# One weight load split in two, two table loads placed where they are used, and the background steps of the first MLP group dealt out over the later ones

## The chip, the cores and the metric

The kernel runs on 1 core of one Trainium2 chip. The metric is the device time of one execution in microseconds (us). Where several executions were timed, the median is given.

## The reference

Two layers of a mixer block over 512 tokens of width 1024, with a context of 256 tokens ahead of them. The cut below keeps what the change touches: the modulation vectors (six per layer, for the tokens from `c` and for the context from `c_ctx`) and the MLP with its squared ReLU.

```python
for l in range(DEPTH):                       # DEPTH = 2
    need_ctx = l < DEPTH - 1
    mx = jnp.split((jax.nn.silu(c) @ w_ada[l] + b_ada[l])[:, None, :], 6, axis=-1)
    mc = jnp.split((jax.nn.silu(c_ctx) @ w_ada[l] + b_ada[l])[None, None, :], 6, axis=-1)
    hx = modulate(rmsnorm(x, g_pre_mix[l]), mx[0], mx[1])
    hc = modulate(rmsnorm(ctx, g_pre_mix[l]), mc[0], mc[1])
    out_x, out_c = token_mixers(hx, hc, ...)   # mLSTM heads, a Fourier mix, a conv module
    x = x + mx[2] * rmsnorm(out_x, g_post_mix[l])
    hx = modulate(rmsnorm(x, g_pre_mlp[l]), mx[3], mx[4])
    x = x + mx[5] * rmsnorm(sq_relu_mlp(hx, w_mlp1[l], w_mlp2[l]), g_post_mlp[l])
    if need_ctx:
        ...                                    # the same for ctx with mc
def sq_relu_mlp(h, w1, w2):
    return jnp.square(jax.nn.relu(h @ w1)) @ w2
```

## The kernel before

All values are fp32. A product is made from three matmuls on halves: weights and activations are each split into a rounded `hi` (an ACT copy, L220 or L231) and a rest `lo` (a DVE subtraction, L221 or L234). A weight block arrives by DMA in a `raw` tile, is split into `hi` and `lo`, and the raw tile is free again. There are 3 raw tiles, 6 hi, 5 lo, 20 tiles called t3, 8 called t4, and two groups of 4 PSUM banks (`mm` and `aux`).

What sets the order: a scheduler takes the program as written, gives each engine one queue and may move an instruction ahead of others in it. Every engine then runs its queue strictly in order and waits on semaphores. All DMAs that move data are issued by SyncE (SP), in one queue. A DMA into a raw tile waits there until the tile's former content has been read, and what is behind it in the queue waits too.

**The start.** `ada_first` (L281 on) computes the first modulation vectors of layer 0 from four quarters of `w_a0`. Each quarter is loaded into the `rooms` of its row (L290); a room of 128x1024 takes two blocks of the contraction, a room called `half_` takes one, in the first 512 columns of a t3 tile. L313 multiplies the blocks on PE with the silu of the conditions (`csil`). The first part of the layer, meanwhile, runs the value projection of the mLSTM (L511) with weights `w_v`. Behind the loads of the context (`ctx`) stand two DMAs that write `csil` column by column into a small table `cd` in DRAM (L587), and one that loads the table `bd` for the Fourier mix (L588). Nothing reads them soon: `bd` is used at L935, and `cd` is read back by L330.

**The MLP of layer 0** takes 768 tokens, 6 blocks of 128, and 32 blocks of 128 hidden columns in 8 groups of 4. Group 0 is plain: L464 multiplies the hidden blocks, `mlp1_out` squares them (L1063, L1064), L1074 multiplies with the second weights, and ACT evicts the result into 6 accumulators (L1238). Between the evictions DVE builds sums of the activations (`sum_steps`, L1108 to L1130), since groups 1 to 7 use a Strassen-like scheme with two pairs of hidden blocks per group (`mlp1_pair`): seven products of 12 matmuls each (L1143) per pair, combined by DVE (L1162, L1170, L1173, L1179) with copies by ACT (L1158, L1169, L1178, L1184). The evictions of these groups are DVE additions (L1242) into the accumulators.

**The background steps.** Layer 1's modulation vectors are computed on DVE (`ada_dve_steps`), in 52 steps: a start that reads the table `cd` back into two t4 tiles, 48 steps that each load 512 KB of `w_at` into a raw tile (L339) and run multiply-and-reduce instructions over it (L343), and three final steps. The 16 steps of the first third have four L343 instructions each, two of which write their unneeded product into an `aux` bank; the other 32 have two. A call of `background()` takes the next steps from the list, two of them per call (L1316). Group 0 calls it four times behind its products (L1202, L1203); groups 1 to 6 call it four times each, at three places in the products and once ahead of the second product with the second weights.

Of the kernel before, what the change touches and what calls it, by code (L numbers as in the profile page):

```python
# [65 lines left out]
def build(tc, a):  # L66
# [156 lines left out]
    def weight(*key, ahead=AHEAD):  # L223
        assert stream[st["used"]][0] == key, (stream[st["used"]][0], key)
        st["used"] += 1
        prep(st["used"] + ahead)
        return ready.pop(key)
# [55 lines left out]
    def ada_first(res):  # L283
        ac = small.tile([128, 4, 8], F32, tag="ac0", name=nm("ac"))
        res["ac", 0] = ac
        raw_ = lambda: rawp.tile([128, 1024], F32, tag="raw", name=nm("raw"))
        hi_ = lambda: hip.tile([128, 1024], F32, tag="hi", name=nm("raw"))
        lo_ = lambda: lop.tile([128, 1024], F32, tag="lo", name=nm("raw"))
        half_ = lambda: t3()[:, :512]
        rooms = ((raw_, raw_, raw_, t4), (hi_, hi_, hi_, lo_), (lo_, raw_, raw_, raw_), (half_,) * 6 + (raw_,))  # L290
        parts = []
        bt = c2()
        for q in range(4):
            parts.append([])
            kb = 0
            for i, r in enumerate(rooms[q]):
                n = 1 if r is half_ else 2
                raw = r().rearrange("p (k j n) -> p k j n", k=n, j=4)
                dma(raw, a["w_a0"][q, kb // 2] if n == 2 else a["w_a0"][q, kb // 2, :, kb % 2:kb % 2 + 1])
                if q == i == 0:  # L300
                    dma(bt, a["bada"][0, 0])
                for k in range(n):
                    parts[q].append(raw[:, k])
                kb += n
            if q < 3:
                pre["v", 0, 0, q] = t3()[:, :264 * (VKB[q][1] - VKB[q][0])]
                dma(pre["v", 0, 0, q].rearrange("p (k n) -> p k n", n=264), a["w_v"][0, 0, :, VKB[q][0]:VKB[q][1], :])
        yield
        for q in range(4):
            ps = aux()  # L310
            for kb in range(KB):
                for j in range(4):
                    T.matmul(ps[32 * j:32 * j + 32, 0:128], csil[:, kb, :], parts[q][kb][:, j, :],  # L313
                             start=kb == 0, stop=kb == KB - 1, tile_position=(0, 32 * j))
            R = bt[:, 128 * q:128 * q + 128]
            V.tensor_tensor(R, ps[:, 0:128], R, ALU.add)
            yield
            cp = aux()
            T.matmul(cp[:, 0:8], R, sel, start=True, stop=True)
            V.tensor_copy(ac[:, q, :], cp[:, 0:8])  # L320
            yield


    def ada_dve_steps(l, res):
        box = {}

        def start():
            box["c"] = [t4() for _ in range(2)]
            for v in range(2):
                dma(box["c"][v], cd[v].partition_broadcast(128))  # L330

        def step(g, j, cb):
            def run():
                if (j, cb) == (0, 0):
                    box["part"] = small.tile([128, 2, 4, 8], F32, tag="part", name=nm("part"))
                    if g:
                        V.memset(box["part"], 0.0)
                w = rawp.tile([128, 2, 512], F32, tag="raw", name=nm("raw"))
                dma(w, a["w_at"][l - 1, g, j, cb])  # L339
                for v in (1, 0) if g == 0 else (0,):  # L340
                    for i in range(2):
                        o = aux() if v else w[:, i, :]
                        V.scalar_tensor_tensor(o, w[:, i, :], 1.0, box["c"][v][:, 512 * i:512 * i + 512],  # L343
                                               ALU.mult, ALU.mult,
                                               accum_out=box["part"][:, i, cb, 2 * j + v:2 * j + v + 1])
            return run

        def fin(g):
            def run():
                ac = small.tile([128, 4, 8], F32, tag=f"ac{g}", name=nm("ac"))  # L350
                res["ac", g] = ac
                part = box["part"]
                bg_ = small.tile([128, 4, 8], F32, tag="bac", name=nm("bac"))
                dma(bg_, a["bcol"][l - 1, g])
                V.tensor_tensor(ac, part[:, 0], part[:, 1], ALU.add)
                V.tensor_tensor(ac, ac, bg_, ALU.add)
                if g:
                    gp = small.tile([128, 8], F32, tag="gp", name=nm("gp"))
                    dma(gp, a["gpcol"][l - 1, g - 1])
                    jv = ac.rearrange("p c (j v) -> p v j c", v=2)[:, 0, 2 * (g - 1):2 * g, :]  # L360
                    V.tensor_tensor(gp.rearrange("p (j c) -> p j c", j=2), gp.rearrange("p (j c) -> p j c", j=2), jv,
                                    ALU.mult)
                    ps = aux()
                    T.transpose(ps[0:8, 0:128], gp, ident)
                    row = small.tile([8, 128], F32, tag="grow", name=nm("grow"))
                    V.tensor_copy(row, ps[0:8, 0:128])
                    dma(gd[l][g - 1][0].rearrange("(k n) -> k n", k=8), row)
            return run
        out = [start]
        for g in range(3):  # L370
            out += [step(g, j, cb) for j in range(4) for cb in range(4)] + [fin(g)]
        return out
# [102 lines left out]
    def layer(l, res, nbg, first=None):  # L475
# [69 lines left out]
        else:  # L545
# [37 lines left out]
                v_out(ps[0, b], 0, b)  # L583
            for b in range(CB):
                xn[b] = unit(ct[b])
            for v in range(2):
                dma(cd[v].rearrange("(k p) -> p k", p=128), csil[:, :, v])  # L587
            dma(bd, a["bd"])  # L588
            some(1, xb, range(2), mm)
            pt = [turned(xn, KORD[m], 1) for m in range(2)]  # L590
            for m in range(KB):
# [358 lines left out]

        for i, (n, j) in enumerate(CHUNKS):
            if n == "f":
                ws = [weight("f", l, k) for k in range(2)]
                four = fourier(ws)
                advance()
                next(four)
                advance()
                background()
                continue
            w = weight(n, l, j)  # L960
            ranges = CX if n == "k" else segs
            outs = stationary(w, ranges)
            advance()
            if n == "t":
                tg[j] = t3()
                for o, (t0, m) in zip(outs, ranges):
                    S.activation(tg[j][:, t0:t0 + m], o[:, :m], AF.Tanh, scale=0.5)
            elif n == "a":
                u[j] = t3()
                for z0 in (0, PAD + CTX, UW - PAD):  # L970
                    P.memset(u[j][:, z0:z0 + PAD], 0.0)
                for o, (t0, m) in zip(outs, ranges):
                    d0 = PAD if t0 == 0 else 2 * PAD + CTX
                    V.scalar_tensor_tensor(u[j][:, d0:d0 + m], tg[j][:, t0:t0 + m], 1.0, o[:, :m], ALU.add, ALU.mult)
                if j == 1:
                    taps = conv_taps()
                    gate_columns()
            elif n == "q":
                got["q"] = short_conv(outs, lambda k: cols[:, C_QK + 8 * k + j:C_QK + 8 * k + j + 1], ranges)
            elif n == "k":  # L980
                got["k"] = short_conv(outs, lambda k: dk[:, k, j:j + 1], ranges)
            elif n == "o":
                to = t3()
                for o, (t0, m) in zip(outs, ranges):
                    S.activation(to[:, t0:t0 + m], o[:, :m], AF.Tanh, scale=0.5)
                staged.append(mlstm(j, got["q"], got["k"], to))
            if taps is not None:
                for _ in range(TAPS):
                    prio = tc.cur_priority
                    tc.cur_priority = prio + LATER  # L990
                    done = next(taps, 1) == 1
                    tc.cur_priority = prio + 1
                    if done:
                        staged.append(conv_norm())
                        taps = None
                        break
            background()
# [194 lines left out]
        for g in range(NF // 4):  # L1192
            gt = [(t3(F32R), t3(F32R)) for f in range(4)]
            ws0, early = None, {}
            if g == 0:

                w1 = [weight("w1", l, f) for f in range(4)]
                for rg in ((0, 256), (256, 256), (512, 256)) if not last else ((256, 256), (512, 256)):
                    for f in range(4):
                        outs = stationary(w1[f], [rg])  # L1200
                        mlp1_out(outs[0], rg[0], rg[1], *gt[f])
                for f in range(4):  # L1202
                    background()  # L1203
                between = sum_steps()
            else:
                one_, two_ = (mlp1_pair(2 * g + i, gt[2 * i], gt[2 * i + 1]) for i in range(2))
# [108 lines left out]
    for l in range(DEPTH):  # L1315
        nxt = []  # L1316
        if l + 1 < DEPTH:
            nxt = ada_dve_steps(l + 1, res[l + 1])
        bgn = background_of(nxt, 2)
        phase = {"mlp": False}  # L1320

        def background(flush=False, l=l, bgn=bgn, phase=phase):
# [154 lines left out]
```

## Time and profile before

| | |
|---|---|
| median of 3 runs | 1514.47 us (1512.51 to 1516.58) |
| the profiled execution, its own time | 1513.57 us |
| its span, first to last instruction | 1511.9 us |
| mean granted TensorE clock | 0.999 |
| PE busy | 1471.7 us, 97% |
| PE weight loads busy | 1292.6 us, 85% |
| DVE busy | 1093.8 us, 72% |
| ACT busy | 757.9 us, 50% |
| POOL busy | 84.4 us, 6% |

The span leaves 1513.57 - 1511.9 = 1.7 us of the profiled execution outside. Times in the rows below are microseconds from the span's start. PE runs the matmuls, DVE is VectorE, ACT is ScalarE, SP issues the DMAs. An "x8" behind an operation means that eight instructions of one line were merged into a row. A bracket such as [1.01 <-DMA raw<-w_v] is idle time of the engine just before the row, and what ended it. Matmuls are pipelined: the distance from one start to the next, not the length of one, is what a matmul costs. The same holds for DVE, where a row's length overlaps the next start a little.

### The profile page before, as it was taken

What the parts mean: (1) busy time and instruction counts of PE and PEld (TensorE: products, weight loads), DVE (VectorE), ACT (ScalarE), POOL (GpSimd) and SP (SyncE); (2) the same over time, 40 slices, a digit from 0 to 9 for tenths busy, and PEclk for the clock granted to TensorE, in tenths of its full rate; (3) what the DMA queues carried; (4) which work ended last, traced back from release to release, by engine and by line L of the source; (5) the groups of instructions that cost most, each with busy time, mean ns of one, the idle gap of its engine ahead of it and who ended that gap; (6) DMA issues with size and microseconds to landing.
All of it is one profiled execution on the core that took longest, in us unless ns stands there. A gap on an engine that the chain in (4) does not pass through costs nothing. (4 is left out here: it accounts for less than half of the span.)

```text
span 1511.9 us, 23296 instructions
## 1 busy us (share of the span) xinstructions
PE 1471.7 (97%) x8894; PEld 1292.6 (85%) x8894; DVE 1093.8 (72%) x2155; ACT 757.9 (50%) x1523; POOL 84.4 (6%) x233
## 2 busy tenths in 40 slices
PE   7899999999999999999999999999999999999997
PEld 4878888987888898898988978888888889998887
DVE  3449987854899886766866576799666977667666
ACT  4632345535745352442524576544557555555544
POOL 0000012200000000000000010011111000000000
PEclk9999999999999999999999999999999999999999
DMA  8645436523532452432622252422225142333234
GB/s 317 156 140 206 158 122 219 207 70 123 183 126 96 144 193 72 166 136 88 195 76 92 80 183 97 133 84 76 107 84 180 43 126 98 112 112 100 83 95 143
DMA packets 68128, 197.32 MB, mean 131 GB/s; under 512 B 14064, under 2 KB 16528, under 8 KB 68016
## 3 DMA queue, kind: packets, MB, share of 16 engines
q1 hardware_dynamic: 66576, 191.11, 37.7%
q0 software_dynamic: 1440, 4.72, 1.0%
q8 instruction: 70, 1.15, 0.3%
q14 instruction: 42, 0.34, 0.1%
HBM read 183.14 MB, written 12.66 MB: 130 GB/s over the span
## 5 line engine op out<-in xcount | busy, mean ns | idle before, releaser
L220 ACT ACTIVATE hi<-raw 128x1024 fp32r<-128x1024 f32 (+1 forms) x245 | 244.0, 1000 | 375.8 <-PE mm L1074 141.6
L1074 PE MATMUL mm<-hi,t 128*128 128x512 f32 (+1 forms) x1296 | 406.4, 392 | 0.1
L221 DVE TENSOR_TENSOR lo<-raw,hi 128x1024 fp32r<-128x1024 f32 (+1 forms) x245 | 280.2, 1146 | 62.7 <-ACT hi L220 28.7
L1074 PEld LDWEIGHTS mm<-hi,t 128*128 128x128 f32 x1296 | 242.3, 188 | 54.9 <-DVE t L234 1.1
L1074 PE MATMUL mm<-lo,t 128*128 128x512 f32 (+1 forms) x648 | 253.4, 391 | 0.0
L464 PE MATMUL mm<-hhi,hi 128*128 128x256 f32 (+1 forms) x576 | 167.9, 336 | 0.0
L464 PE MATMUL mm<-hlo,hi 128*128 128x256 f32 (+1 forms) x576 | 165.8, 332 | 0.0
L464 PE MATMUL mm<-hhi,lo 128*128 128x256 f32 (+1 forms) x576 | 165.2, 331 | 0.0
L1074 PEld LDWEIGHTS mm<-lo,t 128*128 128x128 f32 x648 | 121.9, 188 | 26.3
L1143 PE MATMUL mm<-hhi,hi 128*128 128x384 f32 (+1 forms) x448 | 138.5, 309 | 1.8 <-ACT c L1169 1.7
L1143 PE MATMUL mm<-hhi,lo 128*128 128x384 f32 (+1 forms) x448 | 138.1, 308 | 1.5 <-DVE lo L221 1.5
L1242 DVE TENSOR_TENSOR t<-mm,t 128x512 f32<-128x512 f32 x120 | 81.6, 687 | 78.6 <-PE mm L1074 78.6
L1143 PE MATMUL mm<-hlo,hi 128*128 128x384 f32 (+1 forms) x448 | 138.0, 308 | 0.0
L464 PEld LDWEIGHTS mm<-hhi,hi 128*128 128x128 f32 x576 | 106.7, 188 | 14.9 <-issue 2.9
L464 PEld LDWEIGHTS mm<-hhi,lo 128*128 128x128 f32 x576 | 108.2, 188 | 10.8
L464 PEld LDWEIGHTS mm<-hlo,hi 128*128 128x128 f32 x576 | 107.8, 188 | 11.3 <-issue 0.8
L690 DVE SCALAR_TENSOR_TENSOR t<-t,half,t 128x783 f32<-128x783 f32 (+1 forms) x120 | 101.8, 886 | 0.4
L1143 PE MATMUL mm<-t,hi 128*128 128x384 f32 (+1 forms) x448 | 97.2, 308 | 0.0
L1143 PEld LDWEIGHTS mm<-hhi,hi 128*128 128x128 f32 x448 | 84.2, 188 | 3.9 <-ACT c L1169 2.2
L1143 PEld LDWEIGHTS mm<-hhi,lo 128*128 128x128 f32 x448 | 84.2, 188 | 1.9 <-DVE lo L221 1.9
L234 DVE TENSOR_TENSOR t<-c,t 128x256 fp32r<-128x256 f32 (+1 forms) x132 | 62.1, 477 | 32.5 <-ACT t L231 31.7
L1143 PEld LDWEIGHTS mm<-hlo,hi 128*128 128x128 f32 x448 | 84.2, 188 | 1.2
(254 smaller groups left out, 2706.1 us busy)
## 6 DMA issues: line engine op xcount, KB each, us to landing
raw<-w SPq DMA_DIRECT2D x128, 512.0 KB, 4.1
raw<-w_at SPq DMA_DIRECT2D x48, 512.0 KB, 3.5
raw<-w_a SPq DMA_DIRECT2D x44, 512.0 KB, 4.6
raw<-w_c SPq DMA_DIRECT2D x32, 512.0 KB, 4.2
xd<-t SPq DMA_DIRECT2D x20, 512.0 KB, 3.9
raw<-w_o SPq DMA_DIRECT2D x16, 512.0 KB, 5.3
t<-xd SPq DMA_DIRECT2D x20, 256.0 KB, 6.5
t<-x SPq DMA_DIRECT2D x8, 512.0 KB, 7.8
```

The source lines that it names most:

```text
L220: S.activation(hi[:, r0:n0], raw[:, r0:n0], AF.Copy)
L221: V.tensor_tensor(lo[:, r0:n0], raw[:, r0:n0], hi[:, r0:n0].bitcast(F32), ALU.subtract)
L234: V.tensor_tensor(blk_lo, src, blk_hi.bitcast(F32), ALU.subtract)
L464: T.matmul(o[:, :n], wp[:, k, :], hp[:, k, t0:t0 + n], start=k == 0 and i == 0, stop=k == KB - 1 and i == 2)
L690: V.scalar_tensor_tensor(o, u[j][:, o0 + k:o1 + k], w, o, ALU.mult, ALU.add)
L1074: T.matmul(ps, hp[:, 128 * b:128 * b + 128], wp[:, f % 2, c0:c1], start=f == fs[0] and at[0] == 0 and n == 0, stop=f == fs[-1] and at[1] = ...
L1143: T.matmul(ps[:, :HN], wp[:, K2 * j + k, :], hp, start=first and k == 0 and i == 0, stop=k == K2 - 1 and i == 2, skip_group_check=True)
L1242: V.tensor_tensor(ac_, ps, ac_, ALU.add)
```

## The change

Three edits. First, the fourth quarter of `w_a0` goes into eight half rooms (t3 tiles) instead of six and a raw tile, so its last 512 KB load becomes two of 256 KB. Second, the two writes of the `cd` table move into the first background step, and the load of `bd` moves ahead of the Fourier weights. Third, group 0 of the MLP no longer calls `background()`, and each call in the later groups takes three steps instead of two.

```diff
-        rooms = (..., (lo_, raw_, raw_, raw_), (half_,) * 6 + (raw_,))
+        rooms = (..., (lo_, raw_, raw_, raw_), (half_,) * 8)
...
         def start():
             box["c"] = [t4() for _ in range(2)]
             for v in range(2):
+                dma(cd[v].rearrange("(k p) -> p k", p=128), csil[:, :, v])
                 dma(box["c"][v], cd[v].partition_broadcast(128))
...
-            for v in range(2):
-                dma(cd[v].rearrange("(k p) -> p k", p=128), csil[:, :, v])
-            dma(bd, a["bd"])
             some(1, xb, range(2), mm)
...
             if n == "f":
+                if l == 0:
+                    dma(bd, a["bd"])
                 ws = [weight("f", l, k) for k in range(2)]
...
                         mlp1_out(outs[0], rg[0], rg[1], *gt[f])
-                for f in range(4):
-                    background()
                 between = sum_steps()
...
-        bgn = background_of(nxt, 2)
+        bgn = background_of(nxt, 3)
```

What the scheduler makes of it is seen in the queues. The first place is SP's queue at the start, behind the first loads of `w_a0` (`t_53` and before). `w_a` is here a part of `w_a0`, a name with a number is a tile. Before:

```order
L299 DMA raw_232<-w_a 128x1024
L563 DMA t_62_248<-ctx 128x1024
L563 DMA t_63_249<-ctx 128x1024
L214 DMA raw_595<-w_v 128x792
L214 DMA raw_601<-w_v 128x792
L587 DMA cd<-csil 128x8x1 x2
L588 DMA bd_sb<-bd 128x256
L214 DMA raw_826<-w_v 128x528
L354 DMA bac_5759<-bcol 128x32
```

The same place after the change:

```order
L299 DMA t_54_232<-w_a 128x512
L299 DMA t_55_234<-w_a 128x512
L564 DMA t_63_250<-ctx 128x1024
L564 DMA t_64_251<-ctx 128x1024
L214 DMA raw_597<-w_v 128x792
L214 DMA raw_603<-w_v 128x792
L214 DMA raw_825<-w_v 128x528
L952 DMA bd_sb<-bd 128x256
L330 DMA cd<-csil 128x8x1 x2
L355 DMA bac_5799<-bcol 128x32
```

The load of the last 528 columns of `w_v` has passed the three small DMAs. These stay where they were otherwise: the scheduler issues them as early as it can, whatever place the program gives them.

The second place is DVE's queue near the end of MLP group 1, from the second eviction on. Before:

```order
L1242 TENSOR_TENSOR t_828_4854<-mm_5418,t_828_4854 128x512
L343 SCALAR_TENSOR_TENSOR aux_5447,part_4730<-raw_5445,t_787_4727 128x512
L343 SCALAR_TENSOR_TENSOR aux_5449,part_4730<-raw_5445,t_787_4727 128x512
L343 SCALAR_TENSOR_TENSOR raw_5445,part_4730<-raw_5445,t_786_4726 128x512 x2
L343 SCALAR_TENSOR_TENSOR aux_5455,part_4730<-raw_5453,t_787_4727 128x512
L343 SCALAR_TENSOR_TENSOR aux_5457,part_4730<-raw_5453,t_787_4727 128x512
L343 SCALAR_TENSOR_TENSOR raw_5453,part_4730<-raw_5453,t_786_4726 128x512 x2
L1242 TENSOR_TENSOR t_833_4890<-mm_5469,t_833_4890 128x512
L1242 TENSOR_TENSOR t_844_4932<-mm_5483,t_844_4932 128x512
```

After the change (L344 and L1240 are the same lines under new numbers):

```order
L1240 TENSOR_TENSOR t_805_4793<-mm_5380,t_805_4793 128x512
L344 SCALAR_TENSOR_TENSOR aux_5409,part_5155<-raw_5407,t_867_5150 128x512
L344 SCALAR_TENSOR_TENSOR aux_5411,part_5155<-raw_5407,t_867_5150 128x512
L344 SCALAR_TENSOR_TENSOR raw_5407,part_5155<-raw_5407,t_866_5149 128x512 x2
L344 SCALAR_TENSOR_TENSOR aux_5417,part_5155<-raw_5415,t_867_5150 128x512
L344 SCALAR_TENSOR_TENSOR aux_5419,part_5155<-raw_5415,t_867_5150 128x512
L344 SCALAR_TENSOR_TENSOR raw_5415,part_5155<-raw_5415,t_866_5149 128x512 x2
L344 SCALAR_TENSOR_TENSOR aux_5425,part_5155<-raw_5423,t_867_5150 128x512
L344 SCALAR_TENSOR_TENSOR aux_5427,part_5155<-raw_5423,t_867_5150 128x512
L344 SCALAR_TENSOR_TENSOR raw_5423,part_5155<-raw_5423,t_866_5149 128x512 x2
L1240 TENSOR_TENSOR t_810_4829<-mm_5439,t_810_4829 128x512
```

Between the second and the third eviction of group 1 stand now 12 background instructions where 8 stood. In all, group 1 has 11 steps of four such instructions behind the start step, and group 0 has none.

## Rows read from the trace of the kernel before

**Rows 1.** The page, busy time, share of the span and number of instructions of TensorE

```profile
PE 1471.7 (97%) x8894; PEld 1292.6 (85%) x8894; DVE 1093.8 (72%) x2155; ACT 757.9 (50%) x1523; POOL 84.4 (6%) x233
```

**Rows 2.** Timeline of SP's DMA issues at the start: start, length, engine, line, operation

```profile
38.71 2.56 SPq L587 DMA_DIRECT2D cd<-csil  x2
...
45.83 0.35 SPq L214 DMA_DIRECT2D raw<-w_v  x1
```

**Rows 3.** Timeline of ACT, the same columns, with idle time before a row

```profile
55.06 0.65 ACT L220 ACTIVATE hi<-raw 128x528 fp32r<-128x528 f32 x1 [1.01 <-DMA raw<-w_v]
```

**Rows 4.** Timeline of PE at the start

```profile
17.57 0.90 PE L446 MATMUL aux<-ident_sb,t 128*128 128x128 f32 x3 [1.57 <-ACT t L411]
...
24.85 1.08 PE L313 MATMUL aux<-raw,csil 128*32 128x128 f32 x16
...
45.12 0.64 PE L313 MATMUL aux<-raw,csil 128*32 128x128 f32 x16
...
48.63 0.39 PE L511 MATMUL mm<-hi,hhi 128*128 128x264 f32 x1 [1.81 <-DVE hhi L233]
...
56.80 0.98 PE L446 MATMUL aux<-ident_sb,t 128*128 128x128 f32 x7 [0.68 <-ACT t L411]
```

**Rows 5.** Busy time by MLP group (0, 1, 2 of layer 0): window, then each engine

```profile
404.00:461.60 57.60, 57.60 (x353) 51.37 (x352) 57.22 (x144) 26.62 (x57) 0.00 (x0) 1.00 0.29 94
461.60:527.40 65.80, 63.58 (x313) 56.03 (x312) 59.11 (x118) 29.42 (x47) 0.00 (x0) 1.00 0.39 136
527.40:590.00 62.60, 62.60 (x314) 56.33 (x313) 44.24 (x84) 25.80 (x42) 0.00 (x0) 1.00 0.38 127
```

**Rows 6.** The same windows, busy time of the background instructions (L343) alone

```profile
404.00:461.60 57.60, 19.30 (x56) 1.00 0.29 94
461.60:527.40 65.80, 20.59 (x64) 1.00 0.39 136
527.40:590.00 62.60, 10.78 (x32) 1.00 0.38 127
```

**Rows 7.** Timeline of PE in MLP group 1

```profile
461.62 0.34 PE L1143 MATMUL mm<-hhi,hi 128*128 128x384 f32 x1
...
489.94 0.44 PE L1143 MATMUL mm<-hhi,lo 128*128 128x384 f32 x1 [1.54 <-DVE lo L221]
490.22 0.34 PE L1143 MATMUL mm<-hhi,hi 128*128 128x384 f32 x1
...
491.78 0.39 PE L1074 MATMUL mm<-hi,t 128*128 128x512 f32 x1
...
498.20 0.40 PE L1074 MATMUL mm<-hi,t 128*128 128x512 f32 x1
...
510.50 0.40 PE L1074 MATMUL mm<-hi,t 128*128 128x512 f32 x1
```

**Rows 8.** Timeline of DVE at the end of group 1

```profile
502.02 0.55 DVE L234 TENSOR_TENSOR t<-c,t 128x384 fp32r<-128x384 f32 x1
502.49 0.68 DVE L1242 TENSOR_TENSOR t<-mm,t 128x512 f32<-128x512 f32 x1
503.18 1.23 DVE L221 TENSOR_TENSOR lo<-raw,hi 128x1024 fp32r<-128x1024 f32 x1
504.33 0.68 DVE L1242 TENSOR_TENSOR t<-mm,t 128x512 f32<-128x512 f32 x1
504.93 0.69 DVE L343 SCALAR_TENSOR_TENSOR aux<-raw,t 128x512 f32<-128x512 f32 x1
...
509.89 2.48 DVE L1242 TENSOR_TENSOR t<-mm,t 128x512 f32<-128x512 f32 x4
```

**Rows 9.** The page, DMA issues: count, KB each, median us from issue to landing

```profile
raw<-w SPq DMA_DIRECT2D x128, 512.0 KB, 4.1
raw<-w_at SPq DMA_DIRECT2D x48, 512.0 KB, 3.5
```

**Rows 10.** Line L343 alone: idle time of DVE before it, in us and times

```profile
  DMA raw<-w_at: 10.7, 13
```

More of the change, by code (lines that the diff above doesn't have):

```diff
@@ L289, in ada_first @@
         half_ = lambda: t3()[:, :512]
-        rooms = ((raw_, raw_, raw_, t4), (hi_, hi_, hi_, lo_), (lo_, raw_, raw_, raw_), (half_,) * 6 + (raw_,))
+        rooms = ((raw_, raw_, raw_, t4), (hi_, hi_, hi_, lo_), (lo_, raw_, raw_, raw_), (half_,) * 8)
         parts = []
```

## The prediction

> **What bounds the kernel now.** The page's first part comes first: PE is busy for 1471.7 us, 97% of the span [rows 1]. What PE loses in waits is therefore all that a change in order can win, about 40 us in the whole program, and whatever delays PE's queue adds to the time in full. I then read each place that the change touches: the issues of SP in the first 60 us, with ACT and PE beside them [rows 2 to 4], and the first groups of the MLP, by windows [rows 5, 6] and by single rows of PE and DVE [rows 7, 8]. In group 0 PE is busy for 57.60 of 57.60 us: DVE works there nearly all the time and yet nobody waits for it. In group 1 PE loses 65.80 - 63.58 = 2.2 us, mostly in one wait of 1.54 us for a DVE split [rows 5, 7]. In group 2 it loses nothing. The granted clock is 1.00 in all three.
>
> **The split load.** PE's multiplication with the raw tile that goes away starts at 45.12 with no wait before it [rows 4], because the matmuls in front of it take longer than the load; two loads of 256 KB in place of one of 512 KB gain nothing there, and cost two short issues on a queue whose work lies far ahead of its readers. I take 0. If that cover were gone, the loads would cost at most a landing of 512 KB, 3.5 to 4.1 us [rows 9].
>
> What the edit does change is who gets the raw tile. In the new queue the last `w_v` load stands ahead of `bd` and the two `cd` writes and needs only an early raw tile. Before, it was issued at 45.83, 7.1 us after the first `cd` write at 38.71 [rows 2], and ACT, which splits it, waited 1.01 us for it at 55.06 [rows 3]; through ACT, PE waited 0.68 us at 56.80 [rows 4]. Issued some 6 us sooner it lands before ACT arrives. PE's wait of 0.68 us goes, and PE has no other wait beside it in those rows that would take its place. Gain 0.7 us; bounds 0 (ACT's queue is late for another reason) and 1.0 (all of ACT's wait).
>
> **The two tables.** They do not move to where they are used: in the new queue they stand one load later than before. Both are read hundreds of microseconds later, so that is worth 0 by itself; the cover is the whole first half of the layer.
>
> **Group 0 without background.** 28 instructions of L343 leave (the 56 rows count each with its accumulator read): 19.30 us of DVE at 0.62 us each and some overlap [rows 6]. PE did not wait in this group, so the gain there is 0. The activation sums end earlier, and the weight splits that group 1 needs with them; the 1.54 us wait, and the rest of the 2.2 us, go.
>
> **Group 1 with 44 instead of 32.** Here the steps come back. I followed DVE's new queue from the first addition of a product (L1162) to the third eviction, with pitches from [rows 8]: 44 background instructions at (509.89 - 504.93)/8 = 0.62 us are 27.3; 16 additions and splits of 384 columns at 0.47 are 7.5; 6 splits of 1024 at 1.15 are 6.9; the raw-weight arithmetic, one full row of 1024 and two of 512, is 2.3; three evictions at 0.60 are 1.8. Together 45.8 us. The start is set by PE: 24 matmuls behind the group's first one at 461.62, at the pitch (491.78 - 490.22)/9 = 0.173 us [rows 7], 461.62 + 4.2 + a latency of 0.2 = 466.0. DVE would end at 511.8 without a pause. Three splits wait for weights whose raw tile a background instruction must free first: 4.1 us of landing [rows 9] and 1.05 of ACT's copy against 2 to 5 us of DVE work in between leaves some 1.1 us of pauses in all. So the third eviction ends near 513.0.
>
> PE meanwhile has no wait up to its first matmul with the second weights: 156 products at 0.1735 end at 488.7. Then 72 matmuls with the second weights at (510.50 - 498.20)/53 = 0.232 us [rows 7] and 12 products are 18.8 us, with a pause of 1.1 us for a late ACT split in between: 508.6. The next matmul needs the bank that the third eviction empties. It waits from 508.6 to 513.0, about 4.4 us. Before, the same matmul ran at 510.73, one pitch after 510.50, when its eviction, the first of the four at 509.89, had ended just 0.2 us earlier. So the group loses 513.0 - 510.7 = 2.3 us net, the 2.2 us that it wins already counted. Queued behind the late eviction on DVE are three more evictions and the splits for the second half; PE finds these evictions done in time, one every 0.6 us against 12 matmuls of 2.8 us. Bounds: no pause of DVE, 511.8, +1.1; a pause at each of the four bursts of the mean that DVE waited for `w_at` before, 10.7/13 = 0.82 us [rows 10], +5.6 in all. I take +2.3, because each single load was followed through the queue.
>
> **Group 2 with 32 instead of 16.** DVE had 44.24 us of work in 62.60 [rows 5], 10.78 of it background [rows 6]. Sixteen more at 0.62 make 54.2, so the group holds as a whole, but its first half is denser: the second pair's combination ends about 0.8 us after PE wants its result. I take +0.8, bounds 0 and 3. Groups 3 to 5 take 24 each, 5 us more than before, and end earlier in turn; with 49 of 62.6 us busy I count 0.
>
> **The sum.** -0.7 + 2.3 + 0.8 = +2.4 us. On the profiled execution, 1513.57, that is 1516.0. This execution lies 0.9 us below the median of the runs, 1514.47, so for the median I forecast 1516.9.
>
> **A rule that speaks against it.** PE never stands still for longer than 1.81 us between the point where its rate doubles and the end of the start, at 48.63 [rows 4], and the granted clock stays at 1.00. The pause of 4.4 us forecast above would be longer than any that this trace shows at the full rate. At 24.85, sixteen matmuls of L313 take 1.08 us, at 45.12 the same sixteen take 0.64 [rows 4]: by their ratio the first ran near the lower of the two levels, 1.2 GHz, and the second at the upper, 2.4, and PE had waited before the slow ones, last for over 1 us at 17.57.
>
> The Trainium skill, "TensorE: Matmul & The Clock Gate", section "Part 1: The HAM clock gate (the 'warmup' mystery)", says that the array falls back to 1.2 GHz when it has stood idle and rises again only under steady work. The trace agrees as far as the early slow rows go; no row shows a fall in mid-kernel.
>
> **The rivals.**
> 1. *No new pause.* The third eviction comes by the time PE wants it, at 508.6 plus 0.2, since DVE starts group 1 with less behind it than I counted, or the scheduler's order leaves PE other matmuls. Then group 1 wins 2.2 us, group 2 holds, and the start wins 0.7: 1514.5 - 2.9 = 1511.6. For it speaks that PE lost 2.2 us there [rows 5]; against it, that DVE would have to save 4 of 46 us of queued work. 14%.
> 2. *The clock falls in the pause.* After 4.4 us without work PE runs at 1.2 GHz for a while. At the start the slow rows reach from PE's wait at 17.57 to 24.85 at least, 7.3 us [rows 4]. Matmuls that fill as long a stretch at half rate would have taken half of it: 3.6 us more, 1516.9 + 3.6 = 1520.5, slower than before. It decides if this pause makes the clock fall at all; a wait of 1.81 us did not. 22%.
> 3. *DVE holds PE up in groups 2 to 5.* Three raw tiles hold no fourth load. If in each of these groups one `w_at` landing of 3.5 us [rows 9] stands open behind a burst, and half of it, 1.7 us, reaches PE, the three groups that I counted at 0 cost 5.1 us: 1516.9 + 5.1 = 1522.0. Against it stand 18 us without work on DVE in group 2 [rows 5], of which the added steps take 10. 6%.
> 4. *The change does not do what it says.* The tables do not move, as said. If the start's 0.7 us is then lost in a later wait of the same chain, and groups 1 and 2 come to their low bounds, 1.1 and 0, the time is 1514.5 + 1.1 = 1515.6. 8%.
>
> **How the numbers follow.** The forecast, 1516.9, has 50%; its own range from the bounds is 1514.6 (start -1.0, group 1 at +1.1, group 2 at 0) to 1519.5 (most of the upper bounds; all of them at once would be 1523.1). The range to hold the time 8 in 10 reaches down to 1512 (most of rival 1) and up to 1521 (rival 2). A measurement of this kernel tells some 0.3%, 4.5 us, from no change: faster means below 1509.9, slower above 1519.0. Faster needs a gain that I have not found anywhere: 4%. Slower is rivals 2 and 3, 28%, less 5% for a rival 2 that costs under 2 us, and 4% from the forecast's upper end: 27%. Within is the rest, 69%.
>
> **What would show it.** Right: ACT's wait before the 528-column copy at the start is gone; PE's wait of 1.54 us in group 1 too; one PE wait of 3 to 6 us on the eviction line (new L1240) in group 1, behind a burst of twelve background instructions; a wait under 2 us in group 2 and none in groups 3 to 6. The clock shows in the pitch of the matmuls behind that wait, 0.232 or near 0.46 us. Wrong: no wait on an eviction in group 1 (rival 1), PE waits in each of groups 2 to 5 (rival 3), or a new wait at the start behind the `bd` and `cd` DMAs.

## The result and the profile after

The changed kernel takes 1528.33 us (median of 6 runs, 1524.75 to 1530.15), the kernel before 1515.14 beside it: a ratio of 1.0088, 95% interval 1.0072 to 1.0104, or 13.2 us more. The profiled execution took 1529.5 us with a span of 1527.8, 15.9 us over the span of the execution shown of before. Up to the first product of MLP group 1 it lies 3.4 us behind; a kernel below whose start is that of before (mlp_rate2) lies 3.6 us behind there, so this part is scatter of single executions. Groups 1 to 5 lose 11.3 us, all that follows 1.2.

The first view is the table by windows of the changed kernel: 57.6 us of group 0, then groups 1 to 4, each up to the next group's first product. The columns, as in [rows 5], are window, length, busy time and count of PE, PE loads, DVE, ACT and POOL, granted clock, DMA share and GB/s:

```profile
407.40:465.00 57.60, 57.60 (x348) 51.03 (x347) 46.23 (x92) 29.25 (x59) 0.00 (x0) 1.00 0.15 47
465.00:534.50 69.50, 65.25 (x313) 57.05 (x312) 60.95 (x137) 26.81 (x44) 0.00 (x0) 0.98 0.45 151
534.50:598.80 64.30, 63.45 (x314) 56.08 (x314) 53.44 (x115) 26.13 (x42) 0.00 (x0) 1.00 0.48 156
598.80:665.60 66.80, 63.51 (x315) 56.23 (x314) 48.14 (x94) 26.25 (x42) 0.00 (x0) 1.00 0.45 150
665.60:729.70 64.10, 63.04 (x314) 56.25 (x313) 48.50 (x94) 26.15 (x42) 0.00 (x0) 1.00 0.51 164
```

Group 0, which the steps left, has 11 us less of DVE work than before and the same length: there was nothing to win. Each of the four groups behind it has become longer, and in each PE is short of work, by 4.3, 0.9, 3.3 and 1.1 us. In group 1 the granted clock is 0.98.

What happened in group 1 stands in single rows. First DVE's, with start, length, engine, line and operation:

```profile
505.39 0.68 DVE L1240 TENSOR_TENSOR t<-mm,t 128x512 f32<-128x512 f32 x1
...
507.21 0.68 DVE L1240 TENSOR_TENSOR t<-mm,t 128x512 f32<-128x512 f32 x1
507.81 0.69 DVE L344 SCALAR_TENSOR_TENSOR aux<-raw,t 128x512 f32<-128x512 f32 x1
...
515.27 2.48 DVE L1240 TENSOR_TENSOR t<-mm,t 128x512 f32<-128x512 f32 x4
```

Two evictions (L1240), then the first of twelve background instructions in a row (L344) at 507.81, and the third eviction only at 515.27. PE's rows of the same time, with the idle time before a row in brackets:

```profile
516.10 0.47 PE L1074 MATMUL mm<-hi,t 128*128 128x512 f32 x1 [4.10 <-DVE t L1240]
...
517.12 0.56 PE L1074 MATMUL mm<-lo,t 128*128 128x512 f32 x1
...
519.61 0.63 PE L1074 MATMUL mm<-lo,t 128*128 128x512 f32 x1
520.04 0.89 PE L1074 MATMUL mm<-hi,t 128*128 128x512 f32 x2
520.76 0.39 PE L1074 MATMUL mm<-lo,t 128*128 128x512 f32 x1
```

PE waited 4.10 us for that eviction. The wait of 1.54 us that stood in this group before [rows 7] is gone. From 519.61 to 520.04 one matmul takes 0.43 us in place of the pitch (the distance from one start to the next) of 0.232 worked out from [rows 7]; what the clock did shows in two more windows of the same kernel:

```profile
517.20:520.60 3.40, 3.40 (x10) 2.62 (x9) 3.40 (x6) 0.63 (x1) 0.00 (x0) 0.50 0.31 111
520.70:527.00 6.30, 6.30 (x28) 5.10 (x28) 4.26 (x6) 2.12 (x2) 0.00 (x0) 1.00 0.24 83
```

For 3.4 us the granted clock is 0.50, the lower of the two levels, 1.2 GHz. The nine matmuls from 517.12 to 520.76 take 3.64 us, where nine pitches of 0.232 are 2.09: the fall costs some 1.6 us.

In group 2 PE waits 0.85 us, for ACT's split (L231) in the second pair's combination:

```profile
564.21 0.50 PE L1074 MATMUL mm<-hi,t 128*128 128x512 f32 x1 [0.85 <-ACT t L231]
```

In group 3 the delays pass through several queues. SP's rows come first, with start, how long the issues of the row were spread, and their number; six loads of the steps go out ahead of two weight loads:

```profile
598.66 15.89 SPq L340 DMA_DIRECT2D raw<-w_at  x6
615.95 2.27 SPq L214 DMA_DIRECT2D raw<-w  x2
```

ACT's rows:

```profile
621.57 1.06 ACT L220 ACTIVATE hi<-raw 128x1024 fp32r<-128x1024 f32 x1 [4.26 <-DMA raw<-w]
...
623.65 1.04 ACT L220 ACTIVATE hi<-raw 128x1024 fp32r<-128x1024 f32 x1
...
625.01 0.47 ACT L1169 ACTIVATE c<-mm 128x384 f32<-128x384 f32 x1
```

ACT waits 4.26 us for a weight load, has a second one to copy at 623.65, and only then comes to the copy at 625.01 (L1169). PE's rows there:

```profile
625.53 0.44 PE L1143 MATMUL mm<-hhi,hi 128*128 128x384 f32 x1 [1.52 <-ACT c L1169]
...
639.99 0.27 PE L365 MATMUL aux<-ident_sb,gp 128*8 128x128 f32 x1 [1.77 <-DVE gp L362]
```

PE waits 1.52 us for that copy, and 1.77 us more at 639.99, for a small transposition (L365) that belongs to a background step. What it waits for stands in DVE's rows:

```profile
620.37 0.69 DVE L344 SCALAR_TENSOR_TENSOR raw<-raw,t 128x512 f32<-128x512 f32 x1 [2.51 <-DMA raw<-w_at]
...
638.46 0.68 DVE L1240 TENSOR_TENSOR t<-mm,t 128x512 f32<-128x512 f32 x1
...
639.16 0.68 DVE L344 SCALAR_TENSOR_TENSOR raw<-raw,t 128x512 f32<-128x512 f32 x1
...
639.77 0.16 DVE L362 TENSOR_TENSOR gp<-gp,ac 128x8 f32<-128x8 f32 x1
```

The row at 639.77, 0.16 us long, stands behind an eviction and another background instruction. The load that the row at 620.37 waited 2.51 us for was one of the steps', too.

At the start ACT's wait for the last `w_v` columns [rows 3] is gone:

```profile
55.95 0.66 ACT L220 ACTIVATE hi<-raw 128x528 fp32r<-128x528 f32 x1
```

But PE waits 4.03 us at 49.70, where it waited 1.81 before [rows 4]:

```profile
49.70 0.59 PE L512 MATMUL mm<-hi,hhi 128*128 128x264 f32 x1 [4.03 <-DVE hhi L233]
```

DVE's row behind which that split stands is a copy that was itself held for 3.20 us, by a signal for which the profile names no instruction (`remote`):

```profile
47.92 0.17 DVE L320 COPY ac<-aux 128x8 f32<-128x8 f32 x1 [3.20 <-remote]
```

### The profile page after: what moved, and what is told of

Its sections match the earlier page's. It is cut to its first block, busy times and chain, and to the rows that moved or that the text cites. A ratio compares the mean times of both kernels' runs of the same rounds, so it can differ in the third digit from the quotient of the medians.

```text
span 1527.8 us, 23311 instructions
## 1 busy us (share of the span) xinstructions
PE 1479.3 (97%) x8894; PEld 1296.3 (85%) x8894; DVE 1095.2 (72%) x2155; ACT 760.3 (50%) x1523; POOL 84.5 (6%) x233
## 5 line engine op out<-in xcount | busy, mean ns | idle before, releaser
L1143 PE MATMUL mm<-hhi,hi 128*128 128x384 f32 (+1 forms) x448 | 138.8, 310 | 3.6 <-ACT c L1169 3.6
L1143 PE MATMUL mm<-hhi,lo 128*128 128x384 f32 (+1 forms) x448 | 138.5, 309 | 0.0
L1143 PE MATMUL mm<-hlo,hi 128*128 128x384 f32 (+1 forms) x448 | 138.4, 309 | 0.0
L1240 DVE TENSOR_TENSOR t<-mm,t 128x512 f32<-128x512 f32 x120 | 81.7, 686 | 71.3 <-PE mm L1074 71.2
L465 PEld LDWEIGHTS mm<-hlo,hi 128*128 128x128 f32 x576 | 107.9, 188 | 11.3 <-issue 0.8
L1143 PE MATMUL mm<-t,hi 128*128 128x384 f32 (+1 forms) x448 | 97.4, 309 | 0.0
L1143 PEld LDWEIGHTS mm<-hhi,hi 128*128 128x128 f32 x448 | 84.4, 188 | 5.7 <-ACT c L1169 4.5
L1143 PEld LDWEIGHTS mm<-hlo,hi 128*128 128x128 f32 x448 | 84.4, 188 | 1.2
L1143 PEld LDWEIGHTS mm<-hhi,lo 128*128 128x128 f32 x448 | 84.3, 188 | 0.0
```

What stands on the lines that cost most here:

```text
L465: T.matmul(o[:, :n], wp[:, k, :], hp[:, k, t0:t0 + n], start=k == 0 and i == 0, stop=k == KB - 1 and i == 2)
L1143: T.matmul(ps[:, :HN], wp[:, K2 * j + k, :], hp, start=first and k == 0 and i == 0, stop=k == K2 - 1 and i == 2, skip_group_check=True)
L1240: V.tensor_tensor(ac_, ps, ac_, ALU.add)
```

## The experiments

Twelve kernels, each timed against the kernel before. Beside the ratio the table gives, from each one's profile, the us from the first product (L1143) of a group to that of the next; before, group 1 starts at 461.62 and group 2 at 527.41.

| kernel | ratio, 95% interval | group 1 | 2 | 3 | 4 | 5 |
|---|---|---|---|---|---|---|
| before | | 65.79 | 62.54 | 62.67 | 62.66 | 62.78 |
| the change | 1.0088 (1.0072, 1.0104) | 69.53 | 64.21 | 66.82 | 64.08 | 63.09 |
| start_only | 1.0003 (0.9991, 1.0015) | 65.87 | 62.76 | 63.20 | 62.87 | 62.98 |
| half_only | 1.0013 (0.9999, 1.0027) | 65.52 | 62.75 | 62.99 | 62.87 | 62.98 |
| mlp_only | 1.0072 (1.0050, 1.0093) | 70.54 | 64.10 | 67.95 | 63.77 | 62.72 |
| mlp_rate2 | 0.9978 (0.9967, 0.9990) | 62.78 | 62.60 | 62.60 | 62.61 | 62.71 |
| g0_rate3 | 1.0081 (1.0066, 1.0096) | 75.76 | 65.66 | 64.01 | 62.72 | 62.60 |
| rate_3332 | 1.0033 (1.0020, 1.0045) | 68.57 | 64.96 | 63.21 | 63.05 | 67.91 |
| late_rate3 | 0.9994 (0.9984, 1.0005) | 63.53 | 64.07 | 63.29 | 63.34 | 62.72 |
| late_rate2 | 0.9972 (0.9958, 0.9985) | 62.68 | 62.61 | 62.60 | 62.61 | 62.71 |
| raw4_hi5 | 1.0095 (1.0075, 1.0116) | 73.35 | 63.33 | 63.07 | 62.54 | 62.71 |
| raw4_rate2 | 1.0026 (1.0014, 1.0038) | 62.92 | 67.10 | 63.04 | 62.61 | 62.71 |
| start_rate2 | 0.9986 (0.9974, 0.9997) | 63.06 | 62.76 | 62.98 | 63.42 | 63.10 |
| start_late2 | 0.9997 (0.9984, 1.0009) | 62.98 | 62.76 | 62.98 | 62.80 | 63.09 |

### Which part it is: start_only, half_only, mlp_only

start_only takes the lines of the change at the start and the two table loads, and nothing of the MLP.

```diff
-        rooms = (..., (half_,) * 6 + (raw_,))
+        rooms = (..., (half_,) * 8)
...
-            for v in range(2):
-                dma(cd[v].rearrange("(k p) -> p k", p=128), csil[:, :, v])
-            dma(bd, a["bd"])
...
+                if l == 0:
+                    dma(bd, a["bd"])
```

> Only the two edits at the start, the MLP as before. Theory (the trace after: DVE's L320 copy at 47.9 us waits 3.2 us for a signal while the small writes of cd hold up all DMA traffic, PE then waits 4.0 us, the granted clock falls to 0.50 for 3.4 us): the same wait and fall appear, +2 us, 1516 to 1519. Rival (they belong to that one execution, not to the edits): no such wait, clock 1.00 throughout, the 0.7 us gain that was forecast, 1514 to 1515.

The time is that of the kernel before, within 0.15%. PE's rows at the start show the wait of before, 1.81 us, and no longer one:

```profile
47.20 0.39 PE L512 MATMUL mm<-hi,hhi 128*128 128x264 f32 x1 [1.81 <-DVE hhi L233]
...
48.91 0.42 PE L512 MATMUL mm<-lo,hhi 128*128 128x264 f32 x1
49.13 0.42 PE L512 MATMUL mm<-hi,hhi 128*128 128x264 f32 x1
```

Behind it the clock falls (at 48.91 and 49.13 stand matmuls 0.22 us apart), as the window of the same kernel shows:

```profile
48.00:51.40 3.40, 3.40 (x18) 3.40 (x17) 2.77 (x4) 3.01 (x10) 0.27 (x1) 0.50 0.06 10
```

Before, the same wait of 1.81 us stood there [rows 4] and the clock stayed up. So the fall is no mark of the edits: of the fourteen profiles of this case nine have a fall between 47 and 53 us, and in six of the nine the start is that of before. The wait is less clear. The edits do not bring one of 4 us each time, but of the four profiles with both edits two wait longer here (4.03 and, in start_rate2, 2.43 us), and of the other ten none over 2.00.

half_only has the first of these lines alone.

> Only the last 512 KB load as two half rooms; cd and bd stay ahead of the last w_v load. Theory (what matters is that the half rooms let ctx, w_v and then the cd writes go out some 3 us sooner, so that the stall of the small writes falls on L319 and L320): the 4 us wait of PE and the fall of the clock as in the full change, +2 us. Rival (it is the place of cd and bd behind the last w_v load): as before, 1514 to 1516.

No wait of 4 us and no fall of the clock: in this profile the theory that the line makes them does not come true. The ratio, 1.0013 with an interval of 0.9999 to 1.0027, shows no clear difference.

mlp_only has the rest:

```diff
-                for f in range(4):
-                    background()
...
-        bgn = background_of(nxt, 2)
+        bgn = background_of(nxt, 3)
```

> Only the background steps: none in group 0, three per call later; the start as before. Theory (the MLP holds all the rest: group 1 +3.7 us, group 2 +1.7, group 3 +4.1, group 4 +1.4 by the two traces): 1515 + 11 = 1524 to 1527, with the pause of 4 us on the third eviction of group 1, and a granted clock of 0.50 behind it. Rival (the late arrival from the start shifts DMA landings and so makes part of it): below 1521.

1.0072: nearly all of the loss is in the MLP's part. PE's row on the third eviction repeats the changed kernel's:

```profile
516.19 0.77 PE L1074 MATMUL mm<-hi,t 128*128 128x512 f32 x1 [4.18 <-DVE t L1240]
```

The window around it has the clock at 0.50 for 6.8 us, twice as long as in the changed kernel:

```profile
515.10:521.90 6.80, 5.71 (x14) 4.54 (x15) 6.01 (x12) 1.54 (x2) 0.00 (x0) 0.50 0.37 124
```

In group 3 the wait on L1169 (1.4 us) and that on the transposition (1.9) come back too, the second this time with a fall of the clock (641.4 to 644.8).

### An empty group 0, or three steps per call: mlp_rate2, g0_rate3

mlp_rate2 has one edit against the kernel before: group 0 calls no steps, and the rate stays at two.

```diff
-                for f in range(4):
-                    background()
```

> No background steps in group 0, but two per call as before, so that the steps reach into the last group. Theory (the bursts of three steps ahead of evictions and combinations cost, not that group 0 is empty): bursts of eight instructions as before, no pause on an eviction, no fall of the clock, the 2.2 us of waits in group 1 gone, 1512 to 1515. Rival (steps of four instructions are too many for groups 1 and 2 at any rate per call, or the tail of the steps in groups 6 and 7 costs): 1518 or more.

It is faster than the kernel before. The windows of its groups 1 and 2:

```profile
465.20:528.00 62.80, 62.80 (x314) 56.29 (x313) 52.22 (x105) 27.72 (x45) 0.00 (x0) 1.00 0.42 134
528.00:590.60 62.60, 62.60 (x313) 56.36 (x312) 53.02 (x110) 26.07 (x42) 0.00 (x0) 1.00 0.42 135
```

PE is busy in all of both, with 8.8 us more of DVE work in group 2 than before [rows 5]. The empty group 0 brings 65.79 - 62.78 = 3.0 us.

g0_rate3 is the opposite: group 0 keeps its calls, the rate is three.

```diff
-        bgn = background_of(nxt, 2)
+        bgn = background_of(nxt, 3)
```

> Only the rate: three steps per call, the calls of group 0 stay. Theory (bursts of three are what costs): group 0 takes 11 steps of four instructions without loss, group 1 has five of them and 7 of two, 34 instructions, so no long pause on the eviction, but PE waits of 1 to 2 us on ACT's copies in groups 1 to 3: +3 to +6 us, 1518 to 1522. Rival (an empty group 0 is what costs, because the steps come later): as before, 1514 to 1517.

One number changed from 2 to 3 makes the kernel 0.8% slower, at another place than expected. SP's rows show the DMA queue of the steps and of the weights: start, how long the issues of the row were spread, and their number.

```profile
402.16 35.08 SPq L339 DMA_DIRECT2D raw<-w_at  x10
439.40 39.26 SPq L214 DMA_DIRECT2D raw<-w  x6
```

Ten `w_at` loads for the steps go out in a row, and group 1's weights come behind them. PE's row of what that does:

```profile
471.74 0.69 PE L1143 MATMUL mm<-hhi,lo 128*128 128x384 f32 x1 [6.75 <-DVE lo L221]
```

PE waits 6.75 us for a split of those weights. So the rate costs with steps in group 0 as well as without; my expectation of +3 to +6 us missed that a denser group 0 hits group 1.

### Which burst: rate_3332, late_rate3, late_rate2

rate_3332 is the MLP's part with a rate for each of the four calls in turn.

```diff
-        bgn = background_of(nxt, 3)
+        bgn = background_of(nxt, (3, 3, 3, 2))
```

> None in group 0; of the four calls of each later group the first three take three steps, the last, behind the second pair, two. Theory for group 1 (the third eviction waits behind twelve instructions in place of eight, and the clock falls in that pause): the burst of twelve is one of eight again, 2.5 us shorter, the pause under 2 us, no fall of the clock behind it, group 1 some 4 us shorter than in the full change (65 to 66 us in place of 69.5); the later groups lose 5 to 8 us as before: 1520 to 1525. Rival (the pause comes from the 44 instructions in the whole group, not from the last burst): group 1 stays above 68 us.

DVE's rows: the burst on the way to the third eviction has eight instructions now, but waits in its middle for the steps' own load.

```profile
504.27 0.68 DVE L1240 TENSOR_TENSOR t<-mm,t 128x512 f32<-128x512 f32 x1
504.87 0.69 DVE L343 SCALAR_TENSOR_TENSOR aux<-raw,t 128x512 f32<-128x512 f32 x1
...
508.47 0.70 DVE L343 SCALAR_TENSOR_TENSOR aux<-raw,t 128x512 f32<-128x512 f32 x1 [1.03 <-DMA raw<-w_at]
...
510.96 1.28 DVE L1240 TENSOR_TENSOR t<-mm,t 128x512 f32<-128x512 f32 x2
```

PE's row behind it:

```profile
511.79 0.77 PE L1074 MATMUL mm<-hi,t 128*128 128x512 f32 x1 [2.71 <-DVE t L1240]
```

The pause is 2.71 us in place of 4.1, and the clock falls behind it all the same (511.7 to 515.1). Group 1, at 68.57 us, is where the rival put it, but the pause did get shorter; neither expectation holds in full. In group 5 a step's transposition waits 2.44 us, again with a fall (754.0 to 757.5).

late_rate3 leaves three per call and moves the fourth call of groups 1 to 6 behind the evictions of the first half.

```diff
                 for _ in two_:
                     pass
-                background()
+                if g == NF // 4 - 1:
+                    background()
...
                 for hf in range(2):
+                    if g and hf:
+                        background()
```

> As with the steps' edit alone (none in group 0, three per call), but the fourth call of groups 1 to 6 stands behind the evictions of the first half instead of ahead of them. Theory (the pause of group 1 comes from the burst of twelve instructions between the second and the third eviction, and the fall of the clock from the pause): no pause on the eviction over 1.5 us in group 1, clock 1.00 there, group 1 at 65 to 67 us in place of 69.5 to 70.5; the weight waits of groups 2 to 4 stay: 1519 to 1524. Rival (DVE has too much work in group 1 wherever the burst stands): group 1 at 69 us or more, 1527.

Where the change lost 11.3 us in groups 1 to 5 (327.73 against 316.44), this loses 0.5, and the kernel is level with before, with the same number of steps per call. It still loses some 3.7 us against late_rate2 below, which was timed beside it with two per call (316.95 against 313.21 in these groups, where mlp_only takes 329.08; 1514.09 against 1510.34 in the medians). Its DVE rows in group 1:

```profile
504.83 0.68 DVE L1243 TENSOR_TENSOR t<-mm,t 128x512 f32<-128x512 f32 x1
...
506.59 1.88 DVE L1243 TENSOR_TENSOR t<-mm,t 128x512 f32<-128x512 f32 x3
508.65 0.69 DVE L1243 TENSOR_TENSOR t<-mm,t 128x512 f32<-128x512 f32 x1 [0.18 <-PE mm L1074]
509.26 0.69 DVE L343 SCALAR_TENSOR_TENSOR aux<-raw,t 128x512 f32<-128x512 f32 x1
```

Five evictions are through before the burst at 509.26. PE's longest wait in group 1 is 0.32 us, and the clock stays at 1.00 through the MLP. The waits for weights in group 2 stay (0.93 us), as expected; the two of group 3, 1.5 and 1.8 us, shrink to one of 0.3, which I had not expected.

late_rate2 has the same move at two per call (`background_of(nxt, 2)`).

> None in group 0, two per call, the fourth call behind the evictions of the first half. Theory (at two per call no pause is left on the evictions, so there is nothing to win): the same as at two per call with the calls where they were, ratio 0.997 to 0.999. Rival (the later burst collides with the weight splits of the second half): 1516 or more.

1510.34 us, the fastest of the study; it and mlp_rate2 beat both kernels. Its interval overlaps that of mlp_rate2 and the groups agree to 0.1 us, so no gain of the move shows at two per call.

### The raw tiles: raw4_hi5, raw4_rate2

raw4_hi5 is the MLP's part at three per call, with four raw tiles and, for their room, one tile less for the high halves.

```diff
-C2, T3, T4, HI, LO, RAW = 5, 20, 8, 6, 5, 3
+C2, T3, T4, HI, LO, RAW = 5, 20, 8, 5, 5, 4
```

> The background steps as in the full change (none in group 0, three per call), the start as before, and a fourth raw tile, paid for with one of the six hi tiles. Theory (three steps in one call take all three raw tiles, so the next weights of the MLP wait until DVE has read them, and what follows on ACT and PE is late): the PE waits of group 2 to 4 on ACT's copies (L231, L1169), 3 to 4 us, go or halve; the pause on the third eviction of group 1, which is DVE's own work, stays: 4 to 6 us less than with three raw tiles, 1521 to 1525. Rival (DVE's work alone is the cause, raw tiles do not matter): 1527 to 1530.

Groups 2 to 4 together lose 1.1 us against before (188.94 against 187.87) in place of the change's 7.2, which is what the theory says of a fourth tile. But the time, 1530.87 us, is just above the rival's range. One reason is a pause in group 1, as DVE's rows there show:

```profile
499.85 0.55 DVE L234 TENSOR_TENSOR t<-c,t 128x384 fp32r<-128x384 f32 x1
500.32 0.69 DVE L343 SCALAR_TENSOR_TENSOR aux<-raw,t 128x512 f32<-128x512 f32 x1
...
507.78 1.88 DVE L1240 TENSOR_TENSOR t<-mm,t 128x512 f32<-128x512 f32 x3
```

The whole burst of twelve now stands ahead of the first three evictions. PE's row:

```profile
508.52 0.79 PE L1074 MATMUL mm<-hi,t 128*128 128x512 f32 x1 [7.56 <-DVE t L1240]
```

raw4_rate2 has these pools at two per call.

> None in group 0, two per call, four raw tiles and five hi tiles. A control for the kernel with four raw tiles and three steps per call. Theory (four raw tiles help only where three steps fill them; one hi tile less costs nothing): 1512 to 1515, PE waits in groups 1 to 4 under 1 us in all. Rival (the missing hi tile, or loads that run further ahead, are what made the pause of 7.6 us in group 1 there): a pause on the eviction or on a split of group 1 here too, 1517 or more.

As a control it fails: it, too, has a pause on an eviction, in group 2 now, as PE's row shows, and the clock falls behind it (568.0 to 571.4).

```profile
568.42 0.80 PE L1074 MATMUL mm<-hi,t 128*128 128x512 f32 x1 [2.93 <-DVE t L1240]
```

So these pools move the burst in DVE's order. They also cost time elsewhere: from the first product of group 7 to the first of layer 1's group 1, raw4_hi5 takes 373.9 us and raw4_rate2 373.3, the other twelve profiles 367.5 to 368.8. raw4_hi5 does not settle what three raw tiles cost. That weights wait for their loads is seen in the rows of group 3 above; the tiles' share in the loss is open.

### The start beside the better MLP: start_rate2, start_late2

start_rate2 is mlp_rate2 with the edits of start_only, start_late2 is late_rate2 with them; the edits are shown above.

> Both edits of the start, no steps in group 0, two per call. Theory (the start gives 0.7 to 1 us where the clock does the same in both, the MLP 3 us): 3 to 4 us under the kernel before, ratio 0.997 to 0.998. Rival (the start edits give nothing): the same as the kernel with the rate of two alone, ratio 0.998.

> Both edits of the start, none in group 0, two per call, the fourth call behind the evictions of the first half. Theory (the start edits are worth less than a measurement tells): ratio 0.996 to 0.998, as without them. Rival (they cost 2 us, as the kernel with them and the rate of two came out 0.0008 above the one without): 0.998 to 1.000.

Both came out above the same kernel without the edits of the start, by 0.0008 and 0.0025 of the time; the second is in the rival's range. With start_only at 1.0003 the forecast gain of 0.7 us shows nowhere; only beside late_rate2 do the intervals speak against it. start_late2's profile has a loss that before does not have. ACT's row at 254.61:

```profile
254.61 1.49 ACT L809 ACTIVATE t<-c,pcol 128x256 f32<-128x256 f32 x4 [4.53 <-DMA c<-md]
```

The load of `md` that it waits for lands 8.9 us after its issue. PE's row:

```profile
256.97 0.99 PE L799 MATMUL aux<-t,t 128*128 128x256 f32 x6 [4.05 <-DVE t L812]
```

PE waits 4.05 us, and the clock falls (258.0 to 261.4). The same load takes 5.0 us in the profile of before and 4.9 in late_rate2, but also 6.3 in mlp_only and 7.8 in late_rate3, where the start is untouched. In start_only and start_rate2 PE waits 1.97 and 1.88 us at the same matmuls, each time with a fall behind the wait (256.2 to 259.7 and 257.3 to 260.7); the changed kernel does not wait over 0.6 us there. With the start of before, mlp_only waits 1.14 us and late_rate3 2.50, without a fall. A fall at this place thus stands in three of the four profiles with both edits and in none of the other ten; with one profile of each kernel, whether the edits make it is open.

## Why the prediction was wrong

**Group 1 was right in mechanism and size.** The third eviction was forecast 51.4 us behind the group's first product and ended, at 516.10, 51.1 behind it; the pause was forecast at 4.4 us and was 4.10. The group lost 3.7 us: 2.1 without the clock, where 2.3 stood in the sum. The gain of the empty group 0 that is set off in it was forecast at 2.2 and is 3.0 (mlp_rate2); that the burst's place makes the pause, late_rate3 shows.

**Rival 2, the clock, at 22%, came true**, in the change as in mlp_only and rate_3332. Its price was put at 3.6 us, from the length of the slow rows at the start, and is 1.6 here, for a fall of 3.4 us. In mlp_only the fall of 6.8 us costs 2.7, since its first 1.1 us lie in the pause. The Trainium skill, "TensorE: Matmul & The Clock Gate", section "Part 1: The HAM clock gate (the 'warmup' mystery)", has the array fall to 1.2 GHz when it has stood idle: the traces agree, with 0.50 behind the wait of 4.10 us.

**The step that failed is "Groups 3 to 5 take 24 each, 5 us more than before ... I count 0".** I compared DVE's work with the length of the group, 49 against 62.6 us, and took a group as full or not full. But the order counts, not the sum: mlp_rate2 puts 53 us of DVE work into group 2 without a wait, the change puts 48 into group 3 and loses 4.1 us. Three steps in one call put their instructions and loads in one piece ahead of what PE needs: weights come late on SP, then copies on ACT and splits on DVE. Group 3 lost 4.1 us, group 4 1.4 and group 5 0.3 where 0 stood. Group 2 lost 1.7 where 0.8 stood; the wait that was forecast there came, with 0.85. Of group 3's loss 1.8 us is a wait that I had not looked for at all: a step puts a small transposition into PE's queue, and PE, in order, waits for the DVE chain ahead of it. Rival 3 had a mechanism of this kind at 5.1 us for the three groups and 6%; the price was near, 5.9 us (193.99 against 188.11), the chance far too small. The row that I held against it, DVE idle for 18 us in group 2 [rows 5], says nothing of the order.

**The start** was right in what goes, ACT's wait (none over 0.3 us in the four profiles with both edits), and in that the tables stay at the start. What it brings can't be confirmed: the four pairs of kernels with and without the edits (start_only and before, the change and mlp_only, and the two of the last section) differ by 0.0003, 0.0016, 0.0008 and 0.0025, with half-widths of 0.0012 to 0.0027 (those of a pair's two intervals added in squares). All four are on the slower side, the last alone by more than its half-width. In the profiles the first product of MLP group 1 comes at 465.0 to 466.4 us with both edits, and at 460.5 to 465.2 in the seven with the start and the pools of before: no sign of a gain there either.

**The sum.** The forecast's parts for the MLP came to 2.3 + 0.8 = 3.1 us, against 11.3 in groups 1 to 5. Rival 2 has 1.6 of the rest and rival 3 5.9; what is left, 0.7 us, is nearly all group 2's. The rivals were written as alternatives, but they were parts of one cause, a longer burst per call, and came together. The other 1.9 us of the 13.2 lie outside these groups, within the scatter of the executions.

## What to carry to other kernels

Background work is dealt out by the place of its bursts, not by its total: two steps per call cost nothing in a group with 53 us of DVE work, three cost 12 us in the kernel (g0_rate3). Three per call with the last burst behind the evictions are level with before (late_rate3), but 3.7 us behind two per call (late_rate2): the place was most of the loss, the number of steps the rest. Before moving work on an engine that others wait for, list every instruction in the busiest engine's queue whose producer stands behind a burst, small ones too, and the loads that stand behind the burst's loads. Rivals that share their cause are priced together.

## What the runs showed of the hardware that was not expected

- PE's waits of 2.44 us and more in the MLP (2.44, 2.71, 2.93, 4.10, 4.18, 6.75 and 7.56 us, in six profiles) each have a stretch with the granted clock at 0.50 in them or right behind them; of three of 1.77 to 1.96 us one has. The stretch is 3.4 us, or 6.8 for the waits of 4.18, 6.75 and 7.56. By the starts of the matmuls inside the stretches, such a pause costs its own length and 1.5 to 2.7 us. Elsewhere a wait of that length need not bring a fall: late_rate3's of 2.50 us at 256.84 has none.
- At the start the same wait of 1.81 us is followed by a fall in start_only and by none before. By the pitches of the matmuls of 264 columns, 0.22 us inside the stretch and 0.12 ahead of it, that makes some 1.5 us of the scatter between executions.
- One load (`c<-md`, the same place in the program) takes 4.9 to 8.9 us from issue to landing in the profiles of this study.
- Two small DMAs can be slower than a large one. Two rows of the kernel before, its packets and its issues between 35 and 55 us, with the KB of each and the median us to landing:

```profile
DMA packets 3398, 2.95 MB, mean 147 GB/s; under 512 B 2480, under 2 KB 2608, under 8 KB 3394
...
cd<-csil SPq DMA_DIRECT2D x2, 4.0 KB, 14.0
```

Most of the packets are under 512 B, and a `cd` write of 4 KB takes 14.0 us to land, where 512 KB take 4.1 [rows 9]; how much of the 14.0 is waiting behind earlier loads was not tried.
